# Hybrid decoder block on one core: four weight units instead of three during the first modulation, and the condition's row spread by TensorE

## The chip, the cores and the metric

The kernel runs on one core of a Trainium2 chip. The metric is device time in microseconds (us) of one execution, the median of several. Five engines run side by side, each through its own list of instructions in the order in which it was written: TensorE (PE, with its weight loads PEld), VectorE (DVE), ScalarE (ACT), GpSimd (POOL) and SyncE (SP), which here issues transfers. Each waits on semaphores for the others.

## The reference, cut to what matters

One layer with 512 tokens of width 1024. A conditioning vector `c` gives six vectors by one matrix product; the first two shift and scale the normed input of the token mixer.

```
mod = silu(c) @ ada_w + ada_b
shift1, scale1, gate1, shift2, scale2, gate2 = split(mod, 6)
h = rmsnorm(x, norm1_g) * (1 + scale1) + shift1
proj = h @ w_in + b_in                  # 512 + 2*512 + 2*1024 columns
  pool branch: trailing means of windows 2, 4, 8, 16, a map, a projection
  conv branch: a * sigmoid(a') -> causal depthwise conv, width 31 -> layer norm -> silu -> projection
x = x + gate1 * ((sigmoid(g1) * pool + sigmoid(g2) * conv) @ w_out)
h2 = rmsnorm(x, norm2_g) * (1 + scale2) + shift2
x = x + gate2 * peer(h2)                # 8 heads, top 16 of 128 x 128 product keys, 16384 experts
return rmsnorm(x, final_g)
```

## The kernel before, in words

Activations lie transposed: 8 chunks of 128 channels by 512 tokens. A weight unit is 128 output columns against all 1024 inputs, 128 x 1024 floats (512 KB). It is loaded by SP (`load_unit`, L112), cast to a 16-bit high part on ScalarE (`high`, L117) and to the 16-bit rest on VectorE (`low`, L123). The activation is split in the same way (`hhi`, `hlo`), and a product takes three matmuls (`mm3`, L170 to L172, or `unit`, L179): 24 of 512 columns for a unit. Loads, high and low parts have four buffers each, so the fifth high part needs the first one's buffer back from TensorE.

`w_in` has 28 units. The order of the list `order` begins 8, 4, 9, 5, 0: gate columns of the conv branch (sigmoid, L444), its values (`glu`, L448), and so on. `unit_out` treats a finished unit: it runs the sigmoid, the `glu` or the window sums, takes one step of the other four modulation vectors (`ada_step`: GpSimd multiplies a 512 KB block of `ada_t` with the row of silu(c), L371; ScalarE sums it, L372) and spends a budget of VectorE work from the list `fill`, which holds the depthwise conv, 31 instructions for each of four channel groups (L323, L327). All of it is written out in program order; no scheduler moves it.

The first units (`FU` = 3) are worked on while shift1 and scale1 arrive. For a quarter `q` of the channels, `start_rows(q)` multiplies silu(c), 32 columns wide (`cst`), with two blocks of 1 MB of `ada_n` (L284, `b` = 1 and then `b` = 0) and copies the sums out on ScalarE (L287). `start_turn(q)` turns that row into columns with four small matmuls (L294), and VectorE and ScalarE make `a1`, `shift1`, `hhi` and `hlo` for two chunks (L296 to L303). Then the three units use these two chunks, 6 matmuls each.

The row of silu(c) that GpSimd needs on all partitions, `crow`, is loaded as 128 copies of `c_row` (512 KB) and passed through Silu on ScalarE (L482) in the last quarter.

Of the kernel before, what the change touches and what calls it, by code (L numbers as in the profile page):

```python
# [7 lines left out]
F32 = mybir.dt.float32  # L8
# [3 lines left out]
AF = mybir.ActivationFunctionType  # L12
OP = mybir.AluOpType
# [3 lines left out]
P = 128  # L17
T = 512
D = 1024
NDC = D // P  # L20
# [20 lines left out]
SWE = 15  # L41
WSP = 0.25
ADAB = 3
FU = 3
BUD = 3.6
PL = ()
LNO = (1, 2, 3, 4, 5, 5, 6)
# [17 lines left out]
def body(tc, xt, cols, c_row, ada_n, ada_t, win, pool_w, pup, cvo, wout, wq, keys, ut, un, vn, fg, out, dbg=None):  # L65
    nc = tc.nc
    V, A, G, PE, SP = nc.vector, nc.scalar, nc.gpsimd, nc.tensor, nc.sync
# [11 lines left out]
    def bc_row(ap, n):  # L79
        return bass.AP(tensor=ap.tensor, offset=ap.offset, ap=[[0, P], [1, n]])  # L80
# [5 lines left out]
    def col(name):  # L86
        o, w = COLS[name]
        return colt[:, o:o + w]

    ident = const.tile([P, P], F32, name="ident")  # L90
# [10 lines left out]
    keyt = const.tile([P, 2, P], F32, name="keyt")  # L101
# [8 lines left out]
    def load_unit(src, bufs=4, pool=None):  # L110
        f = (pool or stream).tile([P, 1024], F32, name="unit_f", tag="f32", bufs=bufs)
        SP.dma_start(f, src)  # L112
        return f

    def high(f, scale, bufs=4, pool=None):
        hi = (pool or stream).tile([P, 1024], F16, name="unit_hi", tag="hi", bufs=bufs)
        A.activation(hi, f, AF.Copy, scale=scale)  # L117
        return hi

    def low(f, hi, scale, bufs=4, pool=None, eng=None):  # L120
        lo = (pool or stream).tile([P, 1024], F16, name="unit_lo", tag="lo", bufs=bufs)
        if eng is None:
            V.scalar_tensor_tensor(lo, f, scale, hi, op0=OP.mult, op1=OP.subtract)  # L123
        else:
            A.activation(f, f, AF.Copy, scale=scale)
            eng.tensor_tensor(lo, f, hi, op=OP.subtract)
        return hi, lo
# [7 lines left out]
    def run_ahead(n, nl=4, nh=3, ns=2):  # L135
        for j in range(n, min(n + nl, len(units))):
            if j not in loaded:
                loaded[j] = load_unit(units[j])
        for j in range(n, min(n + nh, len(units))):
            if j not in highs:  # L140
                highs[j] = high(loaded[j], WS)
        for j in range(n, min(n + ns, len(units))):
            if j not in halves:
                halves[j] = low(loaded[j], highs[j], WS, eng=G if j in PL else None)
# [7 lines left out]
    def lows_ahead():  # L152
        run_ahead(used[0], nl=0, nh=0, ns=2)
# [15 lines left out]
    def mm3(o, a, b, start, stop):  # L169
        PE.matmul(o, a[0], b[0], start=start, stop=False)  # L170
        PE.matmul(o, a[0], b[1], start=False, stop=False)  # L171
        PE.matmul(o, a[1], b[0], start=False, stop=stop)  # L172
# [13 lines left out]
    front = fs.enter_context(tc.tile_pool(name="front", bufs=1))  # L186
# [3 lines left out]
    def ps():  # L190
        return psf.tile([P, 512], F32, name="mm", tag="mm", bufs=4)

    def dense(rhs, p=None):
        hi, lo = next_unit()
        p = ps()
        unit(p, hi, lo, [slice(k * P, (k + 1) * P) for k in range(NDC)], rhs)
        return p

    crow = front.tile([P, D], F32, name="crow")

    cst = front.tile([P, NDC, 32], F32, name="cst")
    V.memset(cst, 0.0)
    A.activation(cst[:, :, 0], col("c"), AF.Silu)
    one = front.tile([P, 1], F32, name="one")
    V.memset(one, 1.0)
    mods = [const.tile([P, NDC], F32, name=f"mod{b}") for b in range(6)]
# [2 lines left out]
    def load_ada(u):  # L209
        f = front.tile([P, D], F32, name="ada_f", tag="ada_f", bufs=ADAB)  # L210
        SP.dma_start(f, ada_t[u - 2 * NDC])
        return f
# [35 lines left out]
    def start_load(u):  # L248
        SP.dma_start(spare[u % 5], ada_n[u].rearrange("p (k n) -> p k n", k=NDC))

    pn1 = psf.tile([P, 512], F32, name="ssq", tag="st", bufs=2)
    for k in range(0, NDC, 2):
        SP.dma_start(x_t[:, k:k + 2], xt[:, k:k + 2])
    run_ahead(0, nl=FU, nh=0, ns=0)
    for u in range(5):
        start_load(u)
    for k in range(NDC):
        sq = front.tile([P, 512], F32, name="sq", tag="rstd" if k == 0 else "sql", bufs=1 if k == 0 else 4)
# [4 lines left out]
            V.tensor_tensor(sq0, sq0, sq, op=OP.add)  # L263
    PE.matmul(pn1, ones_d, sq0, start=True, stop=False)
    PE.matmul(pn1, ones_d, sq, start=False, stop=True)
    run_ahead(0, nl=0, nh=FU, ns=FU)
    rstd = front.tile([P, 512], F32, name="rstd")
    A.activation(rstd, pn1, AF.Sqrt, bias=eps)
    b1 = front.tile([P, NDC], F32, name="b1")
# [3 lines left out]

    rows1 = {}

    def start_rows(q):

        p = ps_s.tile([P, 512], F32, name="s_ps", tag="s_ps", bufs=2)
        rows1[q] = front.tile([P, 512], F32, name="row", tag="df", bufs=2)
        for b in (1, 0):  # L280
            u = 2 * q + 1 - b
            for k in range(NDC):
                r = slice(32 * (k % 4), 32 * (k % 4) + 32)
                PE.matmul(p[r, b * 256:(b + 1) * 256], cst[:, k], spare[u % 5][:, k], start=(k < 4), stop=(k >= 4))  # L284
            if u + 5 < NDC:
                start_load(u + 5)
        A.activation(rows1[q], p, AF.Copy)  # L287

    def start_turn(q):

        row = rows1.pop(q)
        for c in range(4):
            b, k = c // 2, 2 * q + c % 2
            PE.matmul(pmod[:, b * NDC + k:b * NDC + k + 1], row[:, c * P:(c + 1) * P], one, start=True, stop=True)  # L294
        s = slice(2 * q, 2 * q + 2)
        V.tensor_tensor(shift1[:, s], pmod[:, s], col("ada_b")[:, s], op=OP.add)  # L296
        V.tensor_tensor(a1[:, s], pmod[:, NDC + 2 * q:NDC + 2 * q + 2], col("norm1_g")[:, s], op=OP.mult)
        V.tensor_tensor(a1[:, s], a1[:, s], b1[:, s], op=OP.add)
        for c in (2 * q, 2 * q + 1):
            V.scalar_tensor_tensor(sig[:, c], x_t[:, c], a1[:, c:c + 1], rstd, op0=OP.mult, op1=OP.mult)  # L300
            A.activation(hhi[:, c], sig[:, c], AF.Identity, bias=shift1[:, c:c + 1])
        for c in (2 * q, 2 * q + 1):
            V.scalar_tensor_tensor(hlo[:, c], sig[:, c], shift1[:, c:c + 1], hhi[:, c], op0=OP.add, op1=OP.subtract)  # L303
# [7 lines left out]
    pw = front.tile([P, 4, P], F32, name="pw")  # L311
# [50 lines left out]
    def ada_load():  # L362
        if nada[0] < 6 * NDC:
            adaf.append((nada[0], load_ada(nada[0])))
            nada[0] += 1
# [73 lines left out]
    def unit_out(n, p):  # L439
        j = order[n]  # L440
        budget = BUD
        if 8 <= j < 12:
            sg = gated[j - 8] = front.tile([P, T], F32, name="sg", bufs=2)
            A.activation(sg, p, AF.Sigmoid, scale=IWS, bias=bin_[:, j:j + 1])  # L444
        elif 4 <= j < 8:
            g = front.tile([P, PADC + T], F32, name="glu", bufs=4)
            G.memset(g[:, :PADC], 0.0)
            V.scalar_tensor_tensor(g[:, PADC:], p, bws[:, j - 4:j - 3], gated[j - 4], op0=OP.add, op1=OP.mult)  # L448
            fill.append(conv(j - 4, g))
            budget -= 0.7  # L450
        elif j < 4:
            wins[j] = windows(j, p)
            after(n + 2, do_df, j)
            after(n + 4, do_map, j)
        else:
            A.activation(sig[:, j - 12], p, AF.Sigmoid, scale=IWS, bias=bin_[:, j:j + 1])
        if n >= FU:
            lows_ahead()
        for f, a in at.get(n, []):
            f(*a)  # L460
            budget -= 0.8
        ada_step()
        ada_load()
        spend(budget, 2)
        if not fill and n > 12 and "c" not in lnorm:
            lnorm["c"] = n
            for k, f in zip(LNO, LN):
                after(n + k, f)
    V.reciprocal(rstd, rstd)
    used[0] = FU  # L470
    outs = [ps() for _ in range(FU)]
    start_rows(0)
    start_turn(0)
    start_rows(1)
    run_ahead(FU, nl=2, nh=0, ns=0)
    SP.dma_start(crow, bc_row(c_row, D))
    SP.dma_start(pw, pool_w)
    SP.dma_start(keyt, keys)
    ada_load()
    for q in range(4):  # L480
        if q == 3:
            A.activation(crow, crow, AF.Silu)  # L482
            run_ahead(FU, nl=2, nh=1, ns=1)
        for j in range(FU):
            hi, lo = halves[j]
            for k in (2 * q, 2 * q + 1):
                s = slice(k * P, (k + 1) * P)
                mm3(outs[j], (hi[:, s], lo[:, s]), (hhi[:, k], hlo[:, k]), k == 0, k == NDC - 1)
            if j == 0 and q < 3:
                start_turn(q + 1)  # L490
            if j == FU - 1 and q < 2:
                start_rows(q + 2)
            if q == 3:
                del halves[j]
                unit_out(j, outs[j])
    dump("hhi", hhi)
# [19 lines left out]
    for u in range(4):  # L516
        for jj, p in enumerate(half((mxhi, mxlo))):
            j = 2 * u + jj
# [16 lines left out]
    for u in range(4):  # L535
        for jj, p in enumerate(half((ychi, yclo))):
            j = 2 * u + jj
# [22 lines left out]
    for j in range(NDC):  # L560
        p = dense((mghi, mglo))
# [164 lines left out]
    for ch in range(17):  # L726
        if ch < 16:
            if ch < 2:
                p = firsts[ch]
            else:  # L730
                hi, lo = next_unit()
                p = q_tile()
# [226 lines left out]
    for g in range(NG):  # L959
        nxt = one_hots(g + 1) if g + 1 < NG else None  # L960
        n = left[0] // (NG - g)
# [253 lines left out]
```

## Time and profile before

| | us |
|---|---|
| median of 3 runs | 1474.02 (1470.59 to 1475.10) |
| profiled execution, its own time | 1472.85 |
| its span in the trace | 1471.1 |
| TensorE busy in it | 1412.7 (96%) |
| VectorE busy | 1270.3 (86%) |
| ScalarE busy | 669.9 (46%) |
| GpSimd busy | 458.3 (31%) |

The shares are means over stages. The change touches the first 60 us; the stage after it, up to about 184 us, is the projection `w_in` with the conv. In it the idle times of VectorE and of TensorE tell more than the shares over the span do. A row's number in brackets is the time that the engine stood idle before it, with what ended that.

### The profile page before, as it was taken

To read this page: it belongs to the slowest core of one execution; us is meant where nothing else is said; L and a number is where in the kernel's file an instruction comes from. 1 tells how busy PE (TensorE), PEld (TensorE's weight loads), DVE (VectorE), ACT (ScalarE), POOL (GpSimd) and SP (SyncE) were. 2 spreads that over 40 slices of the span, in tenths; PEclk is the share of its full clock that TensorE was granted. 3 is DMA by queue.
4 is the path that set the end of the run, shared out by engine and by line. 5 is a ranking of instruction groups with operands and counts; after the bars stand their busy time and mean duration, and the time that the engine had idled before them with its cause. 6 is when DMAs were issued, how large, how long until landed. Compare 5 with 4: busy or idle time off the path is not lost.

```text
span 1471.1 us, 21798 instructions
## 1 busy us (share of the span) xinstructions
PE 1412.7 (96%) x7969; PEld 743.1 (51%) x7969; DVE 1270.3 (86%) x2433; ACT 669.9 (46%) x931; POOL 458.3 (31%) x427
## 2 busy tenths in 40 slices
PE   6998999999989999999999999999999999999997
PEld 2443444445545666665555555555555555444443
DVE  6899966479999999958888988888888898899877
ACT  4554374343433788854333333333333333344334
POOL 0576443200000000000454544445445445422212
PEclk9999999999999999999999999999999999999998
DMA  9554533232233477794899999999999999999953
GB/s 386 192 194 172 185 123 137 79 136 87 72 113 129 150 268 269 249 297 174 295 381 364 371 365 361 375 362 358 366 343 377 364 363 342 357 359 337 326 206 134
DMA packets 145278, 386.79 MB, mean 263 GB/s; under 512 B 10897, under 2 KB 60305, under 8 KB 141073
## 3 DMA queue, kind: packets, MB, share of 16 engines
q1 hardware_dynamic: 108304, 251.15, 48.7%
q0 software_dynamic: 36864, 134.23, 24.8%
q8 instruction: 62, 1.02, 0.3%
q14 instruction: 48, 0.39, 0.1%
HBM read 355.98 MB, written 29.36 MB: 262 GB/s over the span
## 4 chain that ended last, share of the span: by engine, by line
PE 52%; DVE 28%; DMA 7%; issue 6%; POOL 4%; ACT 4%; SPq 0%; POOLq 0%; DVEq 0%; ACTq 0%
PE acc L1093 9%; PE acc L1095 9%; PE acc L1092 9%; DVE unit_lo L123 7%; PE s_ps L172 5%; PE s_ps L170 5%; PE s_ps L171 5%; PE mm L179 4%; DMA gat<-vn,eidx 4%; DVE s_ps L327 3%; POOL gat L987 2%; DVE oh L909 2%; DVE o L907 2%; DVE ol L910 2%; DMA unit_f<-ut 1%
## 5 line engine op out<-in xcount | busy, mean ns | idle before, releaser
L123 DVE SCALAR_TENSOR_TENSOR unit_lo<-unit_f,unit_hi 128x1024 f16<-128x1024 f32 x316 | 397.0, 1266 | 83.9 <-ACT unit_hi L117 80.9
L117 ACT ACTIVATE unit_hi<-unit_f 128x1024 f16<-128x1024 f32 x316 | 330.0, 1046 | 52.9 <-DMA unit_f<-ut 40.4
L987 POOL DMA_INDIRECT gat<-un,eidx x128 | 162.5, 1270 | 586.7 <-DVE bgate L826 421.8
L172 PE MATMUL s_ps<-h2hi,unit_lo 128*128 128x384 f16 x1024 | 334.5, 327 | 7.0 <-DVE unit_lo L123 7.0
L170 PE MATMUL s_ps<-h2hi,unit_hi 128*128 128x384 f16 x1024 | 334.6, 327 | 0.0
L171 PE MATMUL s_ps<-h2lo,unit_hi 128*128 128x384 f16 x1024 | 334.5, 327 | 0.0
L1092 PE MATMUL acc<-unit_hi,ghi 128*128 128x512 f16 x768 | 291.1, 379 | 0.6 <-ACT ghi L1042 0.6
L1093 PE MATMUL acc<-unit_lo,ghi 128*128 128x512 f16 x768 | 291.1, 379 | 0.4 <-DVE unit_lo L123 0.4
L1095 PE MATMUL acc<-unit_hi,glo 128*128 128x512 f16 x768 | 229.9, 379 | 0.1
L987 POOL DMA_INDIRECT gat<-vn,eidx x128 | 158.3, 1236 | 212.0 <-DVE bacc L1011 182.0
L1042 ACT ACTIVATE ghi<-g 128x384 f16<-128x384 f32 x128 | 67.0, 523 | 293.0 <-DVE g L1038 226.8
L1011 DVE SCALAR_TENSOR_TENSOR bacc<-gat,bw,bacc 128x1024 f32<-128x1024 f32 x127 | 162.6, 1280 | 14.9 <-DMA gat<-vn,eidx 14.0
L1003 DVE SCALAR_TENSOR_TENSOR gat<-gat,h2b 128x1024 f32<-128x1024 f32 x128 | 154.4, 1221 | 21.2 <-DMA gat<-un,eidx 20.7
L650 ACT ACTIVATE s_sb<-s_ps 128x384 f32<-128x384 f32 x128 | 63.0, 492 | 222.0 <-PE s_ps L172 211.3
L172 PEld LDWEIGHTS <-unit_lo 128*128 128x128 f16 x1176 | 115.5, 98 | 95.5 <-DVE unit_lo L123 9.2
L171 PEld LDWEIGHTS <-unit_hi 128*128 128x128 f16 x1176 | 115.4, 98 | 85.8 <-issue 3.7
L170 PEld LDWEIGHTS <-unit_hi 128*128 128x128 f16 x1176 | 115.7, 98 | 84.6 <-issue 3.2
L1095 PEld LDWEIGHTS <-glo 128*128 128x128 f16 x768 | 75.0, 98 | 91.6 <-DVE glo L1045 1.5
L1092 PEld LDWEIGHTS <-ghi 128*128 128x128 f16 x768 | 75.1, 98 | 88.4 <-ACT ghi L1042 1.6
L1093 PEld LDWEIGHTS <-ghi 128*128 128x128 f16 x768 | 75.1, 98 | 86.2
L179 PEld LDWEIGHTS <-unit_hi 128*128 128x128 f16 x656 | 64.2, 99 | 91.3 <-ACT unit_hi L117 9.1
L371 POOL TENSOR_TENSOR ada_f<-ada_f,crow 128x1024 f32<-128x1024 f32 x32 | 86.0, 2705 | 69.3 <-ACT crow L482 42.9
(229 smaller groups left out, 1689.4 us busy)
## 6 DMA issues: line engine op xcount, KB each, us to landing
unit_f<-ut SPq DMA_DIRECT2D x128, 512.0 KB
unit_f<-vn SPq DMA_DIRECT2D x128, 512.0 KB
wd<-wst SPq DMA_DIRECT2D x24, 1024.0 KB
wr<-wd SPq DMA_DIRECT2D x16, 1536.0 KB
ada_f<-ada_t SPq DMA_DIRECT2D x32, 512.0 KB
unit_f<-win SPq DMA_DIRECT2D x28, 512.0 KB
unit_f<-wq SPq DMA_DIRECT2D x16, 512.0 KB
sig<-ada_n SPq DMA_DIRECT2D x4, 1024.0 KB
```

Of the source, the lines that this page charges most:

```text
L117: A.activation(hi, f, AF.Copy, scale=scale)
L123: V.scalar_tensor_tensor(lo, f, scale, hi, op0=OP.mult, op1=OP.subtract)
L170: PE.matmul(o, a[0], b[0], start=start, stop=False)
L171: PE.matmul(o, a[0], b[1], start=False, stop=False)
L172: PE.matmul(o, a[1], b[0], start=False, stop=stop)
L179: PE.matmul(p, w[:, s], r[:, k], start=(i == 0 and k == 0), stop=(i == 2 and k == n - 1))
L987: G.indirect_dma_start(out=t, out_offset=None, in_=un if n < HK else vn, in_offset=bass.IndirectOffsetOnAxis(ap=bs["eidx"][:, k:k + 1], ax ...
L1003: V.scalar_tensor_tensor(t, t, 1.0, h2b, op0=OP.mult, op1=OP.mult, accum_out=bs["pre"][:, n:n + 1])
L1011: V.scalar_tensor_tensor(bacc, t, bw[:, k:k + 1], bacc, op0=OP.mult, op1=OP.add)
L1092: PE.matmul(acc[t][h], ghi[:, ts_], vhi[:, h * 512:(h + 1) * 512], start=st, stop=False)
L1093: PE.matmul(acc[t][h], ghi[:, ts_], vlo[:, h * 512:(h + 1) * 512], start=False, stop=False)
L1095: PE.matmul(acc[t][h], glo[:, ts_], vhi[:, h * 512:(h + 1) * 512], start=False, stop=sp)
```

## The change: what it does

`FU` becomes 4, so four units share the quarters. Two units are loaded ahead of the first two `ada_n` blocks, two behind them; the high and low parts of the third and fourth are made after the first quarter's modulation instead of before it. Four more units are queued behind the last `ada_n` block, ahead of `pw`, `keyt` and the `ada_t` blocks. `crow` is no longer loaded: VectorE writes diag(silu(c)) into it, and TensorE multiplies it with a tile of ones (`spread`, eight matmuls of 128 columns in two halves); ScalarE copies the result back. The first half stands between the two halves of `start_rows(0)`, the second behind the small matmuls of `start_turn(0)`. `start_rows(q + 1)` now stands behind the first unit of quarter `q`, `start_turn(q + 1)` behind the second. In the last quarter the parts of units 4 and 5 are written behind the matmuls of units 0 and 1.

```diff
-FU = 3
+FU = 4
     A.activation(cst[:, :, 0], col("c"), AF.Silu)
+    V.tensor_tensor(crow.rearrange("p (k n) -> p k n", k=NDC), cst[:, :, 0:1].to_broadcast([P, NDC, P]),
+                    ident[:, None, :].to_broadcast([P, NDC, P]), op=OP.mult)
...
+    run_ahead(0, nl=2, nh=0, ns=0)
+    start_load(0)
+    start_load(1)
     run_ahead(0, nl=FU, nh=0, ns=0)
-    for u in range(5):
+    for u in range(2, 5):
         start_load(u)
...
-    run_ahead(0, nl=0, nh=FU, ns=FU)
+    run_ahead(0, nl=0, nh=2, ns=2)
...
     V.reciprocal(rstd, rstd)
     used[0] = FU
     outs = [ps() for _ in range(FU)]
-    start_rows(0)
-    start_turn(0)
-    start_rows(1)
-    run_ahead(FU, nl=2, nh=0, ns=0)
-    SP.dma_start(crow, bc_row(c_row, D))
-    SP.dma_start(pw, pool_w)
-    SP.dma_start(keyt, keys)
-    ada_load()
+    ones = front.tile([P, P], F32, name="ones", tag="pt", bufs=2)
+    V.memset(ones, 1.0)
+    def spread(h):
+        for k in range(4 * h, 4 * h + 4):
+            PE.matmul(outs[2 + h][:, k % 4 * P:(k % 4 + 1) * P], ones, crow[:, k * P:(k + 1) * P], start=True, stop=True)
+    start_rows(0, spread)
+    start_turn(0, spread)
+    for h in range(2):
+        A.activation(crow[:, h * 512:(h + 1) * 512], outs[2 + h], AF.Copy)
+    run_ahead(0, nl=0, nh=FU, ns=FU)
     for q in range(4):
-        if q == 3:
-            A.activation(crow, crow, AF.Silu)
-            run_ahead(FU, nl=2, nh=1, ns=1)
         for j in range(FU):
             hi, lo = halves[j]
...
-            if j == 0 and q < 3:
+            if q < 3 and j == 0:
+                start_rows(q + 1)
+                if q == 0:
+                    run_ahead(FU, nl=4, nh=0, ns=0)
+                if q == 1:
+                    SP.dma_start(pw, pool_w)
+                    SP.dma_start(keyt, keys)
+                    ada_load()
+            if q < 3 and j == 1:
                 start_turn(q + 1)
-            if j == FU - 1 and q < 2:
-                start_rows(q + 2)
             if q == 3:
+                if j < 2:
+                    run_ahead(FU, nl=2, nh=j + 1, ns=j + 1)
```

How TensorE's list begins, before (-) and now (+): `s_ps` is the sum of `start_rows`, `pmod` the small matmuls, `mm<-crow,ones` the spread.

```order
-L284 MATMUL s_ps<-sig,cst 32x256 x16
-L294 MATMUL pmod<-one,row 128x1 x4
-L284 MATMUL s_ps<-yc,cst 32x256 x8
-L284 MATMUL s_ps<-h2hi,cst 32x256 x8
+L290 MATMUL s_ps<-sig,cst 32x256 x8
+L489 MATMUL mm<-crow,ones 128x128 x4
+L290 MATMUL s_ps<-sig,cst 32x256 x8
+L302 MATMUL pmod<-one,row 128x1 x4
+L489 MATMUL mm<-crow,ones 128x128 x4
 L170 LDWEIGHTS unit_hi
 L170 MATMUL mm<-hhi,unit_hi 128x512
```

The sums of the second quarter (`yc`, `h2hi`) have moved behind the first unit's matmuls, and the spread stands among those of the first quarter.

VectorE's list at the same place, with what each instruction waits for. Now:

```order
L276 SCALAR_TENSOR_TENSOR b_170<-colt 128x8 [waits DMAHW0_49]
L317 TENSOR_SCALAR dwk<-colt 128x124
L319 TENSOR_SCALAR bws<-colt 128x4
L479 RECIPROCAL rstd<-rstd 128x512 [waits Activation_49]
L484 MEMSET ones 128x128
L306 TENSOR_TENSOR mod_108<-pmod,colt 128x2 [waits PE_49]
```

Before, L296 (now L306) followed the reciprocal directly; the tile of ones is new, and it is written behind the reciprocal.

The end of the last quarter on ScalarE: `sg` is the first unit's sigmoid, `ada_f` a summing step. Before:

```order
L482 ACT_TABLE_LOAD
L482 ACTIVATE crow<-crow 128x1024 [waits DMAHW2_49]
L117 ACTIVATE unit_hi<-unit_f 128x1024 [waits DMAHW0_49]
L444 ACT_TABLE_LOAD
L444 ACTIVATE sg<-mm,colt 128x512 [waits PE_49]
```

Now:

```order
L117 ACTIVATE unit_hi<-unit_f 128x1024 [waits DMAHW1_49,PE_49]
L454 ACT_TABLE_LOAD
L454 ACTIVATE sg<-mm,colt 128x512 [waits PE_49]
L382 ACTIVATE ada_f,mod_110<-ada_f 128x1024 [waits Pool_49]
L117 ACTIVATE unit_hi<-unit_f 128x1024 [waits DMAHW2_49,PE_49]
L382 ACTIVATE ada_f,mod_110<-ada_f 128x1024 [waits Pool_49]
```

The Silu is gone, and both high parts, those of units 4 and 5, now wait for TensorE (for the buffers of units 0 and 1); before, the one high part there waited for its transfer alone. On VectorE the two low parts stand ahead of the first `glu` (L458); before, one did (`L123`, then L448).

## Rows read from the trace of the kernel before

**Rows 1.** The page's first line: span and instructions.
```profile
span 1471.1 us, 21798 instructions
```

**Rows 2.** Stages: start to end, length, busy us of each engine, clock, DMA share, GB/s.
```profile
40.00:50.00 10.00, 9.99 (x51) 5.00 (x50) 6.03 (x9) 7.49 (x9) 3.71 (x3) 1.00 0.07 26
100.00:180.00 80.00, 74.73 (x337) 32.94 (x335) 79.31 (x97) 39.04 (x60) 47.23 (x27) 1.00 0.52 177
180.00:190.00 10.00, 7.82 (x31) 3.26 (x32) 6.60 (x7) 5.71 (x10) 3.42 (x2) 1.00 0.32 92
```

**Rows 3.** Timeline of VectorE: start, us, line, operation; in brackets idle before.
```profile
16.07 3.35 DVE L469 RECIPROCAL rstd<-rstd 128x512 f32<-128x512 f32 x1 [0.48 <-ACT rstd L268]
...
29.89 1.42 DVE L303 SCALAR_TENSOR_TENSOR hlo<-sig,mod,hhi 128x512 f16<-128x512 f32 x2
...
47.18 2.54 DVE L123 SCALAR_TENSOR_TENSOR unit_lo<-unit_f,unit_hi 128x1024 f16<-128x1024 f32 x1 [2.56 <-ACT unit_hi L117]
49.64 0.74 DVE L448 SCALAR_TENSOR_TENSOR glu<-mm,bws,sg 128x512 f32<-128x512 f32 x1
...
59.13 1.22 DVE L123 SCALAR_TENSOR_TENSOR unit_lo<-unit_f,unit_hi 128x1024 f16<-128x1024 f32 x1
...
60.92 1.22 DVE L123 SCALAR_TENSOR_TENSOR unit_lo<-unit_f,unit_hi 128x1024 f16<-128x1024 f32 x1
...
71.00 1.24 DVE L123 SCALAR_TENSOR_TENSOR unit_lo<-unit_f,unit_hi 128x1024 f16<-128x1024 f32 x1 [0.41 <-ACT unit_hi L117]
...
87.49 2.70 DVE L123 SCALAR_TENSOR_TENSOR unit_lo<-unit_f,unit_hi 128x1024 f16<-128x1024 f32 x1 [0.41 <-ACT unit_hi L117]
```

**Rows 4.** Timeline of TensorE, the first 60 us.
```profile
13.09 1.91 PE L265 MATMUL ssq<-sq,ones_d 128*128 128x512 f32 x2
...
17.97 1.07 PE L284 MATMUL s_ps<-sig,cst 128*32 128x256 f32 x16 [0.97 <-DMA sig<-ada_n]
19.75 1.05 PE L294 MATMUL pmod<-one,row 128*128 128x1 f32 x8 [0.72 <-ACT row L287]
...
22.95 1.70 PE L284 MATMUL s_ps<-h2hi,cst 128*32 128x256 f32 x16 [1.14 <-DMA h2hi<-ada_n]
24.57 0.61 PE L170 MATMUL mm<-hhi,unit_hi 128*128 128x512 f16 x1
...
26.90 0.95 PE L294 MATMUL pmod<-one,row 128*128 128x1 f32 x8
27.71 0.38 PE L170 MATMUL mm<-hhi,unit_hi 128*128 128x512 f16 x1
...
30.39 1.07 PE L284 MATMUL s_ps<-h2lo,cst 128*32 128x256 f32 x16
...
47.69 1.89 PE L179 MATMUL mm<-hhi,unit_hi 128*128 128x512 f16 x8
...
51.14 1.89 PE L179 MATMUL mm<-hhi,unit_lo 128*128 128x512 f16 x8
56.43 2.69 PE L179 MATMUL mm<-hhi,unit_hi 128*128 128x512 f16 x8 [3.40 <-ACT unit_hi L117]
```

**Rows 5.** Timeline of ScalarE, the first 60 us.
```profile
14.05 1.28 ACT L268 ACT_TABLE_LOAD   x1
15.35 0.69 ACT L268 ACTIVATE rstd<-ssq,eps 128x512 f32<-128x512 f32 x1
...
22.09 1.38 ACT L301 ACTIVATE hhi<-sig,mod 128x512 f16<-128x512 f32 x2 [2.39 <-DVE sig L300]
...
48.46 0.69 ACT L444 ACTIVATE sg<-mm,colt 128x512 f32<-128x512 f32 x1
49.05 1.05 ACT L372 ACTIVATE ada_f<-ada_f 128x1024 f32<-128x1024 f32 x1
```

**Rows 6.** Chain of waits at 291 us: start, length, what.
```profile
291.30 2.60 PE nat L586 x20
```

**Rows 7.** Timeline of GpSimd, from 40 us.
```profile
46.28 2.35 POOL L371 TENSOR_TENSOR ada_f<-ada_f,crow 128x1024 f32<-128x1024 f32 x1 [42.85 <-ACT crow L482]
```

More of the change, by code (lines that the diff above doesn't have):

```diff
@@ L274, in body, with start_rows @@
     rows1 = {}
-    def start_rows(q):
+    def start_rows(q, wait=None):
         p = ps_s.tile([P, 512], F32, name="s_ps", tag="s_ps", bufs=2)
@@ L284, in start_rows @@
                 PE.matmul(p[r, b * 256:(b + 1) * 256], cst[:, k], spare[u % 5][:, k], start=(k < 4), stop=(k >= 4))
+            if wait and b:
+                wait(0)
             if u + 5 < NDC:
@@ L287, in start_rows, with start_turn @@
         A.activation(rows1[q], p, AF.Copy)
-    def start_turn(q):
+    def start_turn(q, wait=None):
         row = rows1.pop(q)
@@ L294, in start_turn @@
             PE.matmul(pmod[:, b * NDC + k:b * NDC + k + 1], row[:, c * P:(c + 1) * P], one, start=True, stop=True)
+        if wait:
+            wait(1)
         s = slice(2 * q, 2 * q + 2)
```

## The prediction

> **What bounds the kernel now.** I read the stages first, then the timelines of the engines over the first 60 us. From 100 to 180 us VectorE is busy 79.31 of 80 us, TensorE 74.73, ScalarE 39.04 [rows 2]: the projection stage is VectorE's, and this holds until its busy share falls, in 180 to 190 us (6.60 of 10). The reader is to see that this begins much earlier. The first `glu` on VectorE starts at 49.64 us with no idle before it, and after it the timeline shows two waits of 0.41 us, at 71.00 and 87.49 [rows 3]. So from 49.64 us on VectorE works through the conv and the low parts almost without a pause, and the end of the stage lies as late as that start plus the work behind it. TensorE's visible loss, 3.40 us of idle at 56.43 and then matmuls that ran slower (8 in 2.69 us against 1.89) [rows 4], lies beside this run of VectorE. Whoever removes it gains only if VectorE also begins earlier or has less to do. What the change is worth is therefore the start of the first `glu`, less the VectorE work taken out from behind it.
>
> **The start, step by step.** The order shows that the first half of the spread stands on TensorE between the two halves of the first sums, and that it needs the tile of ones, which VectorE writes behind the reciprocal. Both lists run in order, so nothing passes it.
>
> The last matmul of the norm runs from 13.09 for 1.91 us, to 15.0 [rows 4]. The square root started at 15.35, behind a table load from 14.05 to 15.33 [rows 5]; with one high part less ahead of it (1.05 us, the size of the row at 49.05 [rows 5]) the table is loaded by 14.3, and the root can start at 15.05. Its 0.69 us [rows 5], the reciprocal's 3.35 [rows 3] and some 0.2 for the fill give ones at 19.3 us. TensorE waits there. The four products are eight passes; the nearest row with 128 x 128 floats has 20 passes in 2.60 us, 0.13 each [rows 6], so 1.05 us, to 20.4. Then the second half of the sums, 1.07 us, which before started at 17.97 when its transfer landed [rows 4]: it ends at 21.5 instead of 19.04. One unit less is loaded ahead of these blocks; two blocks of 1 MB landed between 17.97 and 22.95 [rows 4], so 512 KB are 1.25 us. That is thus worth nothing: the second block is there at 16.7 and waits for the spread. The second half of the spread (1.05 us) costs nothing; it lies in the 3.05 us between the sums' end (19.04) and the first `hhi` (22.09 [rows 5]), of which the small matmuls take 1.05.
>
> Before, the second quarter's sums came next and ended at 24.57, where the first unit began [rows 4]. Now the first unit goes ahead of them. From the sums' end to the start of the small matmuls are 0.71 us (19.04 to 19.75 [rows 4]); from that start to the end of the two `hlo` 4.4 us (26.90 on TensorE, 29.89 + 1.42 on VectorE [rows 3, 4]). So `hlo` is whole at 26.6, the first unit's six matmuls end at 27.0, the second quarter's sums (two times 1.07 [rows 4]) at 29.1, the second unit's six at 30.4; a matmul costs 0.216 us, from 16 between 47.69 and 51.14 [rows 4]. ScalarE in the meantime copies `crow` back (twice the 0.69 us of 512 columns) and makes two high parts (twice 1.05), all behind `hhi`, which ends at 25.95: it is free at 29.4 and copies the second row by 30.1, just in time. VectorE's two low parts lie in its wait, too.
>
> **The quarters.** A quarter now takes 24 matmuls (5.18 us), its sums (2.1), the gap that the small matmuls make (26.90 to 27.71, 0.81 [rows 4]): 8.1 us. The way round from the small matmuls to the end of `hlo` is 4.4 us against 3.4 of matmuls and gap before the next quarter begins and 4.26 before it needs the last `hlo`; I add 0.05. The small matmuls of quarters 1 and 3 start at 30.4 and 46.7, and the first unit ends 4.4 + 0.4 us later, at 51.5.
>
> One more thing lies in this stretch. `crow` is ready at 27, so GpSimd no longer waits until 46.28 for it [rows 7]; it multiplies as soon as the first `ada_t` block lands. The bytes up to there are those that before had landed by about 40.7 (the transfers fill 0.07 of 40 to 50 us [rows 2]; one 512 KB broadcast is gone, one unit more is loaded ahead, and two more stand before the first of these blocks). The multiplies of 2.35 us thus run from 40.7 to about 48, and VectorE makes `sig` and `hlo` of the third quarter from 40 to 43. The low part at 47.18, begun 0.9 us into such a multiply, took 2.54 us instead of 1.22 [rows 3, 7], 1.3 more. From below the collision costs 0, from above the rest of one multiply, 2.35; I take 1.5, nearest to the row, and the first unit ends at 53.0.
>
> The Trainium skill ("SBUF — State Buffer", section "Who interferes with whom") says that a VectorE instruction with two SBUF inputs contends with a GpSimd instruction that reads SBUF, and that the loser blocks for the whole of the other. By it a collision costs up to the full 2.35 us, and the sum would be 0.85 higher; the low part at 47.18, which ends 1.1 us after the multiply, agrees [rows 3, 7]. By the same section the conv's instructions, whose running sum is in PSUM, lose nothing to GpSimd, so that starting the multiplies early gives nothing back there.
>
> **The end of the quarters.** Before, the Silu with its two table loads delayed the first sigmoid to 48.46. That goes, but the four buffers are now all in work: high(4) waits for the first unit's end, and VectorE's order puts low(4) and low(5) ahead of the first `glu`. From 53.0 on ScalarE: high(4) 1.05, a table load 1.28, the sigmoid 0.59 (48.46 to 49.05), the summing step 1.1, high(5) 1.05 [rows 5]; then low(5), 1.22 [rows 3]: 6.3 us, so the first `glu` starts at 59.3 instead of 49.64, 9.7 later. Less two low parts that before stood behind it (59.13 and 60.92, 1.15 from start to next start, 2.3 [rows 3]), less the two waits of 0.41, since ScalarE then has a lead over VectorE: 9.7 - 2.3 - 0.8 = 6.6 us later at the end of the stage. TensorE's removed idle time should come back as a wait for low parts. Behind the stage nothing is taken out, and what follows waits for the conv; I give back nothing. `crow`'s diag on VectorE lies in its wait for the squares, the four queued loads in transfers that would come anyway.
>
> **The sum.** The profiled execution took 1472.85 us, its span 1471.1 [rows 1], 1.75 around it, which stays; with 6.6 it is 1479.5. The median of the runs is 1.2 above the profiled one; on it the sum is 1480.6. I predict 1480.0.
>
> **Rivals.** First, TensorE sets the end. For it speaks its 74.73 of 80 us [rows 2] and that the 3.40 us and the slow matmuls are real. Then what counts is when the fifth unit ends: before at 63.3 (56.43, 24 matmuls, and 1.7 for the slow clock, worked out in the third rival); now four units end at 53.0 + 3.9 and the fifth, without a wait, at 62.1: 1.2 less, 1471.7 to 1472.8. Had the spread not held the start back (5.2 us, the second rival), 1467. Against it: VectorE's 79.31 of 80 us. It decides where the low parts are ready before TensorE asks for them.
>
> Second, the spread holds nothing up (ones or root come earlier than I reckon). Sums end at 17.8, the first unit at 47.8 with no collision, the first `glu` at 54.1: 4.5 - 3.1 = +1.4, 1475.4. Against it: the order. For it: nothing but that ends of matmuls are modelled.
>
> Third, worse: the clock falls inside the quarters. After 1.14 us of idle the sums at 22.95 took 1.70 us instead of 1.07, and the six matmuls from 24.57 to 26.90 2.33 instead of 1.29, in all 1.7 us; after 3.40 us of idle, eight took 2.69 instead of 1.89 [rows 4]. TensorE now stands idle for over 2 us before 19.3, and again before its first matmul. If the slow stretch falls where TensorE is the limit, 1.7 us come on top, and a second blocked multiply 2.35: 1484.
>
> **Chances.** The forecast 0.55, and its own range, from no collision to a full one and with 1.5 for errors in the chain, 1477 to 1483; TensorE sets the end 0.17; the spread free 0.13; worse 0.15. The range that should hold 8 in 10 reaches down into the first rival and takes in the third: 1472.5 to 1485.5. A measurement of this kernel tells about 0.3% from no change, 4.4 us: slower is above 1478.4. Of the forecast 0.43 lies above that and 0.12 below; of the worst case 0.13 above, 0.02 below; the free spread is no change, at 0.13; TensorE's case is no change with the start held back (0.09) and faster without (0.08). That makes faster 0.08, same 0.36, slower 0.56.
>
> **What would show it.** TensorE idle before the spread until about 19.3; the sums' second half at about 20.4; the first unit's matmuls from about 25; the first `glu` at 58 to 60.5; VectorE full from there to about 190, where now it is 184; TensorE waiting for low parts at unit 6. A first `glu` before 56, or a VectorE with pauses of more than 3 us behind it, would make the prediction wrong.

## The result, and the profile after

The changed kernel takes 1485.11 us (median of 4 runs, 1483.72 to 1487.49) against 1474.56 (4 runs, 1470.59 to 1475.34) for the kernel before: a ratio of 1.0075, 95% interval 1.0057 to 1.0094. It is slower by 10.5 us. Forecast were 1480.0 us and a range of 1472.5 to 1485.5. The direction held, and so did the engine that sets the end; two prices on the way to it did not, and the loss is nearly twice the forecast.

The span, and two stages of it (start to end, length, busy us of TensorE, its weight loads, VectorE, ScalarE, GpSimd, then granted clock, DMA share, GB/s):

```profile
span 1483.0 us, 21832 instructions
```

```profile
100.00:180.00 80.00, 76.39 (x337) 33.19 (x336) 79.57 (x101) 40.24 (x61) 49.91 (x33) 0.98 0.53 183
180.00:190.00 10.00, 10.00 (x48) 4.42 (x46) 9.79 (x14) 5.71 (x9) 1.83 (x3) 1.00 0.53 178
```

VectorE still fills the projection stage (79.57 of 80 us), and where it was falling off, at 180 to 190, it now works 9.79 of 10 us [rows 2]. The stage only lies later. Its timeline shows from where:

```profile
16.03 3.35 DVE L479 RECIPROCAL rstd<-rstd 128x512 f32<-128x512 f32 x1 [1.11 <-ACT rstd L274]
19.36 0.17 DVE L484 MEMSET ones<- 128x128 f32 x1
...
44.39 5.38 DVE L313 SCALAR_TENSOR_TENSOR hlo<-sig,mod,hhi 128x512 f16<-128x512 f32 x2
...
58.14 1.41 DVE L313 SCALAR_TENSOR_TENSOR hlo<-sig,mod,hhi 128x512 f16<-128x512 f32 x2
61.11 1.23 DVE L123 SCALAR_TENSOR_TENSOR unit_lo<-unit_f,unit_hi 128x1024 f16<-128x1024 f32 x1 [1.56 <-ACT unit_hi L117]
65.09 1.23 DVE L123 SCALAR_TENSOR_TENSOR unit_lo<-unit_f,unit_hi 128x1024 f16<-128x1024 f32 x1 [2.75 <-ACT unit_hi L117]
66.23 0.75 DVE L458 SCALAR_TENSOR_TENSOR glu<-mm,bws,sg 128x512 f32<-128x512 f32 x1
```

The first `glu` starts at 66.23 instead of 49.64 [rows 3], 16.6 us later, and behind it VectorE stands idle no more than 0.16 us at a time up to the conv's end. In the third quarter two `hlo` that usually take 1.41 took 5.38. GpSimd's timeline at that moment:

```profile
43.73 2.75 POOL L381 TENSOR_TENSOR ada_f<-ada_f,crow 128x1024 f32<-128x1024 f32 x1 [40.29 <-DVE sig L310]
46.42 0.12 POOL L457 MEMSET glu<- 128x30 f32 x1
46.49 5.49 POOL L381 TENSOR_TENSOR ada_f<-ada_f,crow 128x1024 f32<-128x1024 f32 x2
```

The three multiplies, which began at 46.28 before [rows 7], now begin at 43.73 and cover the two `hlo` from 44.39 on. TensorE's timeline:

```profile
15.20 1.67 PE L290 MATMUL s_ps<-sig,cst 128*32 128x256 f32 x16
19.57 1.82 PE L489 MATMUL mm<-crow,ones 128*128 128x128 f32 x8 [2.70 <-DVE ones L484]
21.33 1.94 PE L290 MATMUL s_ps<-sig,cst 128*32 128x256 f32 x16
...
29.53 0.63 PE L172 MATMUL mm<-hhi,unit_lo 128*128 128x512 f16 x1
...
33.27 0.95 PE L302 MATMUL pmod<-one,row 128*128 128x1 f32 x8
...
41.41 0.95 PE L302 MATMUL pmod<-one,row 128*128 128x1 f32 x8
...
47.07 0.38 PE L171 MATMUL mm<-hlo,unit_hi 128*128 128x512 f16 x1 [1.89 <-DVE hlo L313]
...
49.83 0.38 PE L171 MATMUL mm<-hlo,unit_hi 128*128 128x512 f16 x1 [1.94 <-DVE hlo L313]
50.35 1.74 PE L290 MATMUL s_ps<-sig,cst 128*32 128x256 f32 x16
51.84 1.95 PE L290 MATMUL s_ps<-yc,cst 128*32 128x256 f32 x16
...
55.16 0.95 PE L302 MATMUL pmod<-one,row 128*128 128x1 f32 x8
```

Three things are to be seen. TensorE waits 2.70 us for the ones, as forecast. What follows the wait is slow: the sums at 21.33 take 1.94, against 1.07 at full clock [rows 4]. And the period of the quarters, 8.14 us from 33.27 to 41.41, becomes 13.75 from there to 55.16.

### The profile page after: what moved, and what is told of

It reads as the page before. It is cut to its first block, busy times and chain, and to the rows that moved or that the text cites. A ratio compares the mean times of both kernels' runs of the same rounds, so it can differ in the third digit from the quotient of the medians.

```text
span 1483.0 us, 21832 instructions
## 1 busy us (share of the span) xinstructions
PE 1421.3 (96%) x7985; PEld 746.1 (50%) x7985; DVE 1274.1 (86%) x2435; ACT 668.9 (45%) x931; POOL 455.4 (31%) x427
## 4 chain that ended last, share of the span: by engine, by line
PE 57%; DVE 29%; DMA 5%; issue 4%; ACT 3%; POOL 2%; SPq 0%; DVEq 0%; ACTq 0%; POOLq 0%
PE acc L1116 9%; PE acc L1114 9%; PE acc L1113 9%; DVE unit_lo L123 7%; PE s_ps L172 6%; PE s_ps L170 6%; PE s_ps L171 6%; DVE s_ps L337 5%; PE mm L179 3%; DMA gat<-vn,eidx 2%; DVE oh L930 2%; DVE ol L931 2%; DVE o L928 2%; ACT unit_hi L117 1%; PE q_ps L171 1%
## 5 line engine op out<-in xcount | busy, mean ns | idle before, releaser
L123 DVE SCALAR_TENSOR_TENSOR unit_lo<-unit_f,unit_hi 128x1024 f16<-128x1024 f32 x316 | 396.6, 1265 | 85.6 <-ACT unit_hi L117 84.9
L381 POOL TENSOR_TENSOR ada_f<-ada_f,crow 128x1024 f32<-128x1024 f32 x32 | 82.5, 2595 | 83.4 <-DMA ada_f<-ada_t 43.1
```

## Experiments

All in the table but the changed kernel were timed in five rounds beside the kernel before. "Conv end" is the start of ScalarE's copy of the last conv sum. The row for the changed kernel is that of the first section.

| kernel | first `glu` at | conv end | median us (runs) | ratio to before, 95% |
|---|---|---|---|---|
| before | 49.64 | 184.29 | 1474.25 (23); 1473.67 (23); 1473.38 (15) | |
| changed | 66.23 | 198.35 | 1485.11 (4) | 1.0075 (1.0057 to 1.0094) |
| ones early | 59.06 | 190.95 | 1478.03 (12) | 1.0024 (1.0014 to 1.0033) |
| GpSimd held | 60.97 | 193.59 | 1481.46 (6) | 1.0041 (1.0026 to 1.0057) |
| before, VectorE late | 64.45 | 200.78 | 1490.52 (5) | 1.0107 (1.009 to 1.0123) |
| before, TensorE late | 49.78 | 188.28 | 1475.72 (12) | 1.0011 (1.0001 to 1.0021) |
| early, parts behind | 54.44 | 189.99 | 1477.05 (9) | 1.0031 (1.002 to 1.0043) |
| held, clock kept | 57.79 | 190.88 | 1479.49 (6) | 1.0046 (1.0031 to 1.0061) |
| three units | 47.15 | 182.10 | 1468.32 (9) | 0.9969 (0.9957 to 0.9982) |
| two units | 45.60 | 181.86 | 1469.06 (12) | 0.9967 (0.9956 to 0.9977) |
| four units, all remedies | 51.73 | 187.34 | 1474.03 (11) | 1.0005 (0.9996 to 1.0014) |

**Which engine sets the end: VectorE late, TensorE late.** Both start from the kernel before. One puts 12 instructions on VectorE ahead of the first `glu`, the other the matmuls of one more unit on TensorE. The added work changes no value that the kernel uses.

```diff
+            if n == 1:
+                for _ in range(12):
+                    V.tensor_tensor(rstd, rstd, rstd, op=OP.max)
             V.scalar_tensor_tensor(g[:, PADC:], p, bws[:, j - 4:j - 3], gated[j - 4], op0=OP.add, op1=OP.mult)
```

```diff
     for n in range(FU, len(order)):
+        if n == 5:
+            x = psf.tile([P, 512], F32, name="extra", tag="st", bufs=2)
+            for i in range(24):
+                PE.matmul(x, hhi[:, i % NDC, :P], hhi[:, i % NDC], start=(i == 0), stop=(i == 23))
         unit_out(n, dense((hhi, hlo)))
```

> The kernel before the change with one edit: twelve extra instructions of VectorE (128 x 512, about 0.65 us each, 8 us in all, more where GpSimd blocks them) ahead of the first glu; nothing else is touched. Theory (VectorE sets the end of the projection stage): the first glu starts 8 us or more later than 49.6 and the time grows by the same amount, to about 1482.5. Rival (TensorE sets the end, VectorE has room): the time grows by less than 3 us.

> The kernel before the change with one edit: 24 extra matmuls of 512 columns (5.2 us) on TensorE ahead of the sixth unit. Theory (TensorE has room in the projection stage): the time stays within 1.5 us of the kernel before. Rival (TensorE sets the end, as the removal of its 3.4 us of idle time would need): the time grows by about 5 us, to 1479.7.

VectorE's 12 instructions, then TensorE's 24 matmuls, and VectorE's two longest waits in the run with these:

```profile
49.65 14.88 DVE L450 TENSOR_TENSOR rstd<-rstd 128x512 f32<-128x512 f32 x12
```

```profile
63.27 5.34 PE L501 MATMUL extra<-hhi 128*128 128x512 f16 x24
```

```profile
79.08 0.75 DVE L448 SCALAR_TENSOR_TENSOR glu<-mm,bws,sg 128x512 f32<-128x512 f32 x1 [0.73 <-PE mm L179]
...
92.23 2.69 DVE L123 SCALAR_TENSOR_TENSOR unit_lo<-unit_f,unit_hi 128x1024 f16<-128x1024 f32 x1 [2.52 <-ACT unit_hi L117]
```

14.88 us on VectorE moved the first `glu` by 14.8, the conv's end by 16.5 and the time by 16.3. The 12 took longer than was reckoned for them: the first three, beside GpSimd's multiplies, 2.72 to 2.83 us each, the others, behind these, 0.69; the shift is read from what they took. 5.34 us on TensorE moved the median by 1.5 (0.15 to 3.1). The traced execution, at 1479.65 the longest of the 12, shows more: there the conv's end lies 4.0 later, and VectorE waits 0.73 us for a `glu`'s matmuls and 2.52 for a high part. So VectorE sets the end, and TensorE has room for part of the 5.34 us: by the median for most of it, by this trace for far less. The rival in which TensorE sets the end, so that all of the 5.34 us comes out in the time, falls; how soon still more work on TensorE would make it the bound stays open.

**The wait for the ones.** The changed kernel, with the tile of ones filled at the start, in a buffer of its own, instead of behind the reciprocal:

```diff
+    ones = front.tile([P, P], F32, name="ones")
+    V.memset(ones, 1.0)
     one = front.tile([P, 1], F32, name="one")
...
-    ones = front.tile([P, P], F32, name="ones", tag="pt", bufs=2)
-    V.memset(ones, 1.0)
```

> The changed kernel with one edit: the tile of ones is filled at the start, ahead of the squares, instead of behind the reciprocal. Theory (the first glu on VectorE sets the end of the projection stage, one for one): TensorE no longer stands at 16.9 to 19.6 us, the first quarter's sums end about 3.2 us earlier, at 20 instead of 23.3, and if the two blocked hlo of the third quarter cost the same 4 us as now, the first glu starts at 63 instead of 66.2 and the time falls by about 3.2 us, to 1482. Rival (the start's wait is given back at the third quarter, where the multiplies of GpSimd run at a fixed time set by the transfers): the glu stays within 1 us of 66 and so does the time. Second rival (TensorE sets the end): the glu moves and the time does not.

The time fell by 7.1 us and the first `glu` came 7.2 earlier, twice what was expected. TensorE no longer waits for the ones, and the spread and the sums run at full speed; then, below, the third quarter's `hlo` on VectorE and GpSimd's first multiply:

```profile
16.17 1.16 PE L489 MATMUL mm<-crow,ones 128*128 128x128 f32 x8
17.26 1.07 PE L292 MATMUL s_ps<-sig,cst 128*32 128x256 f32 x16
```

```profile
39.82 1.42 DVE L315 SCALAR_TENSOR_TENSOR hlo<-sig,mod,hhi 128x512 f16<-128x512 f32 x2
```

```profile
42.61 2.36 POOL L383 TENSOR_TENSOR ada_f<-ada_f,crow 128x1024 f32<-128x1024 f32 x1 [39.17 <-DMA ada_f<-ada_t]
```

The `hlo` are over at 41.24 and the multiply begins at 42.61, when its transfer lands: this collision is gone too. The early ones removed two terms at once, since the `hlo` came 4.6 us earlier (44.39 to 39.82) and GpSimd's first multiply, which waits for a transfer, only 1.1 (43.73 to 42.61). But the multiplies now meet the fourth quarter's two `sig`:

```profile
47.38 3.46 DVE L312 SCALAR_TENSOR_TENSOR sig<-x_t,mod,rstd 128x512 f32<-128x512 f32 x2
```

The next two runs take the collision and the clock one after the other.

**The collision alone.** The changed kernel, with one copy on GpSimd that reads the last `hlo` and so holds its multiplies until then:

```diff
     for q in range(4):
+        if q == 3:
+            held = front.tile([P, 1], F32, name="held")
+            G.tensor_copy(held, hlo[:, NDC - 1, 0:1])
         for j in range(FU):
```

> The changed kernel with one edit: GpSimd first copies one column of the last hlo of the fourth quarter, so that its multiplies of ada_t blocks begin only when VectorE has made all hlo. Theory: the two hlo of the third quarter take 1.4 us again instead of 5.4, TensorE does not stand there and its slow sums behind it (1.5 us) go as well; the first glu starts 4 to 5.5 us earlier, at 61 to 62, and the time falls by as much, to 1480 to 1481. Rival (the multiplies are late now and hold up ScalarE's summing steps and high parts behind them): the glu moves little, or VectorE waits later for high parts, and the time falls by less than 2 us.

```profile
44.52 1.41 DVE L313 SCALAR_TENSOR_TENSOR hlo<-sig,mod,hhi 128x512 f16<-128x512 f32 x2
```

The `hlo` of the third quarter take 1.41 again and the first `glu` comes 5.26 earlier, as expected; the time falls by 3.65, a little less than the 4 to 5.5 expected.

**The clock alone.** The kernel just told of, with ten matmuls, whose result is overwritten, in TensorE's wait for the ones:

```diff
+        if h == 0:
+            for i in range(10):
+                PE.matmul(outs[0], halves[0][0][:, :P], halves[0][0][:, :512], start=True, stop=True)
         for k in range(4 * h, 4 * h + 4):
```

> The version with GpSimd held, and ten matmuls of 512 columns, whose results nobody reads, between the first half of the sums and the spread, while TensorE would wait for the ones. Theory (the low granted clock behind that wait lengthens the spread, the second half of the sums and the first unit): the eight spreads take about 1.05 us and the second half of the sums 1.07 (1.8 and 1.94 with GpSimd held alone), the first glu starts 1.5 to 2 us before 60.97, and the time is about 1479.5 to 1480 (1481.46). Rival (the low clock there is hidden by other engines): first glu and time as with GpSimd held alone.

The spread and the sums behind it, with GpSimd held alone and then in this run:

```profile
19.28 1.22 PE L489 MATMUL mm<-crow,ones 128*128 128x128 f32 x8 [2.44 <-DVE ones L484]
20.43 1.94 PE L290 MATMUL s_ps<-sig,cst 128*32 128x256 f32 x16
```

```profile
19.09 1.16 PE L492 MATMUL mm<-crow,ones 128*128 128x128 f32 x8 [0.31 <-DVE ones L484]
20.18 1.07 PE L290 MATMUL s_ps<-sig,cst 128*32 128x256 f32 x16
```

Stages of 4 us with the granted clock as the third number from the end, of the changed kernel, then with GpSimd held alone, then of this run:

```profile
18.00:22.00 4.00, 2.42 (x16) 1.93 (x20) 1.52 (x2) 0.00 (x0) 0.00 (x0) 0.74 1.03 426
...
26.00:30.00 4.00, 2.74 (x7) 0.65 (x5) 2.71 (x5) 3.69 (x6) 0.00 (x0) 0.59 1.01 422
...
52.00:56.00 4.00, 4.00 (x35) 2.04 (x28) 0.00 (x0) 0.60 (x1) 0.05 (x1) 0.75 0.00 0
```

```profile
22.00:26.00 4.00, 3.28 (x17) 2.92 (x14) 0.95 (x4) 0.60 (x1) 0.00 (x0) 0.50 1.02 424
26.00:30.00 4.00, 3.66 (x11) 1.25 (x9) 2.71 (x5) 3.77 (x6) 0.00 (x0) 0.50 1.01 420
```

```profile
18.00:22.00 4.00, 2.97 (x29) 1.58 (x27) 1.04 (x2) 0.60 (x1) 0.00 (x0) 1.00 1.03 427
22.00:26.00 4.00, 2.54 (x18) 2.04 (x19) 2.75 (x7) 1.70 (x3) 0.00 (x0) 1.00 1.01 422
26.00:30.00 4.00, 4.00 (x42) 1.73 (x41) 2.83 (x3) 3.14 (x5) 0.00 (x0) 1.00 1.01 422
```

In the changed kernel TensorE spent part of each of these stretches at the lower of its two levels, 1.2 instead of 2.4 GHz, after it had waited, and with GpSimd held alone all of 22 to 30 us; with the wait filled it stays at full clock. In this pair of traces the spread itself hardly changes (1.22 us and 1.16; the 1.8 of the expectation is the changed kernel's); what gains are the sums (1.94 to 1.07) and what follows them. The first `glu` comes 3.18 us earlier than with GpSimd held alone, and the time falls by 1.97 (1481.46 to 1479.49). The ones come no earlier here, so this is the price of the clock behind the wait; what the wait costs by its own length no run shows alone. With early ones the small matmuls of quarter 1 start another 1.5 us earlier (28.69 against 30.22).

The length of a wait alone does not tell whether the clock falls. TensorE's waits for the first and the last quarter's `hhi` in the run with early ones, and the stretches around them:

```profile
22.15 0.38 PE L170 MATMUL mm<-hhi,unit_hi 128*128 128x512 f16 x1 [1.06 <-ACT hhi L313]
...
50.98 0.38 PE L170 MATMUL mm<-hhi,unit_hi 128*128 128x512 f16 x1 [2.44 <-ACT hhi L313]
```

```profile
22.00:26.00 4.00, 3.44 (x18) 1.06 (x21) 2.71 (x5) 3.62 (x6) 0.00 (x0) 0.57 1.01 422
...
50.00:54.00 4.00, 2.61 (x12) 1.12 (x12) 2.32 (x5) 2.52 (x4) 0.00 (x0) 1.00 0.00 0
```

Behind 1.06 us the granted clock was 0.57, behind 2.44 us it stayed at 1.00; and in the run with the clock kept the same wait for the first `hhi`, 1.05 us, was followed by 1.00.

**The parts of units 4 and 5.** Early ones, and the two high and low parts written behind the second unit's output:

```diff
             if q == 3:
-                if j < 2:
-                    run_ahead(FU, nl=2, nh=j + 1, ns=j + 1)
                 del halves[j]
                 unit_out(j, outs[j])
+                if j == 1:
+                    run_ahead(FU, nl=2, nh=2, ns=2)
```

> The early ones, and the high and low parts of units 4 and 5 written behind the second unit's output instead of ahead of the first. Theory (the start of the first glu moves the end one for one): on ScalarE and VectorE one high part, one wait for it and one low part go from ahead of the first glu, so that it starts at about 54.3 us where the early ones alone had 59.06; the two low parts that now stand behind it give 2.3 us of this back: time about 1475.5 to 1476, 2 to 2.5 us under the early ones alone (1478.03). Rival (TensorE then waits for the low part of unit 4, so that nothing is gained): the first glu starts earlier, but the time stays at 1478.

The first `glu` came 4.62 earlier, as expected, but the conv's end and the time only by 1.0. VectorE's timeline from the first `glu` on, and then a wait of TensorE:

```profile
54.44 0.75 DVE L460 SCALAR_TENSOR_TENSOR glu<-mm,bws,sg 128x512 f32<-128x512 f32 x1 [2.05 <-PE mm L172]
...
59.19 4.08 DVE L123 SCALAR_TENSOR_TENSOR unit_lo<-unit_f,unit_hi 128x1024 f16<-128x1024 f32 x2
```

```profile
62.19 1.90 PE L179 MATMUL mm<-hhi,unit_lo 128*128 128x512 f16 x8 [1.72 <-DVE unit_lo L123]
```

The two low parts are back behind it, and beside one of GpSimd's multiplies (58.70, 2.35 us) they take 4.08 us, not the 2.3 expected. TensorE waits 1.72 us for one of them, as the rival said, but VectorE waits no more than 0.2 us behind its first `glu`. A start of `glu` that only changes places with other VectorE work is no gain; the rule "one for one" holds for the same work behind it.

**Fewer units.** From the kernel before: three units as before, the spread with early ones instead of the loaded `crow`, the next parts and the sigmoid's table load in the third quarter, GpSimd held. The two-unit version differs in `FU` = 2, and in two further buffers for the spread. Of the edit, the part in the quarters (the spread is left out):

```diff
...
     for q in range(4):
+        if q == 2:
+            run_ahead(FU, nl=4 - FU, nh=4 - FU, ns=4 - FU)
+            A.activation(warm, eps, AF.Sigmoid)
         if q == 3:
-            A.activation(crow, crow, AF.Silu)
-            run_ahead(FU, nl=2, nh=1, ns=1)
+            held = front.tile([P, 1], F32, name="held")
+            G.tensor_copy(held, hlo[:, NDC - 1, 0:1])
```

> The kernel before with three units in work, as it had, condition's row spread by TensorE from early ones, the parts of the next unit written in the third quarter, the sigmoid table loaded there, and GpSimd's multiplies held until the last low half of the shifts. Theory (the start of the first glu moves the end one for one): the table load and one high and low part go from ahead of the first glu: it starts at about 46.5 us (before 49.64), and the time falls by about 3 to 1471. Rival (TensorE sets the end of the stage, or the moved parts delay the quarters by as much): 1474 or more.

> The same as the three-unit version, with two units in work while the first shift and scale arrive, and the parts of units 2 and 3 written in the third quarter. Theory: each quarter is shorter by one unit's six matmuls, and the first unit ends at about 42.3 us; the first glu starts at about 43.7 to 44 us, 5.5 us before that of the kernel before, and the time falls to about 1468.7. Rival (TensorE sets the end, and the work that it doesn't do in the quarters comes behind): 1474 or more.

Both beat the kernel before by 0.3% and do not differ from each other. With three units the first `glu` starts at 47.15, where the expectation said 46.5; the conv's end lies 2.2 earlier than before and the median 5.4 lower, so that the start of the `glu` does not explain the whole gain (some of it may lie in the stage told of under the rest of the span). With two units the `glu` starts at 45.60, later than the 43.7 to 44 expected, and the conv's end is only 0.24 earlier than with three. The stretch from 48 to 72 us, three units and then two, and a wait of VectorE in the latter:

```profile
48.00:72.00 24.00, 22.58 (x106) 10.07 (x105) 23.64 (x29) 15.05 (x23) 15.91 (x11) 1.00 0.79 285
```

```profile
48.00:72.00 24.00, 24.00 (x113) 10.89 (x112) 22.10 (x31) 12.56 (x19) 15.70 (x11) 1.00 0.63 227
```

```profile
68.15 1.25 DVE L123 SCALAR_TENSOR_TENSOR unit_lo<-unit_f,unit_hi 128x1024 f16<-128x1024 f32 x1 [1.41 <-ACT unit_hi L117]
```

With three units VectorE is full there (23.64 of 24 us), with two TensorE is (24.00), and VectorE waits. Here the rival seems to set in: two units put so little of TensorE's work in front that it becomes the bound for a while. That is read from these rows; no run tests it.

**Four units with all remedies.** Early ones and parts behind, as above, and in addition the table load in the third quarter and GpSimd held:

```diff
     for q in range(4):
+        if q == 2:
+            A.activation(warm, eps, AF.Sigmoid)
+        if q == 3:
+            held = front.tile([P, 1], F32, name="held")
+            G.tensor_copy(held, hlo[:, NDC - 1, 0:1])
         for j in range(FU):
```

> Four units in work with every remedy found so far: early ones, the parts of units 4 and 5 behind the first glu, the sigmoid table loaded in the third quarter, GpSimd's multiplies held until the last low half of the shifts. Theory (the start of the first glu moves the end one for one, and a fourth unit in the quarters costs what its own matmuls take): the fourth quarter's low halves follow the third's by the undisturbed period, 8.15 us, instead of 10.26, so that the first glu starts at about 52.3 us (54.44 without the last two remedies) and the time is about 1475, some 6 us over the three-unit version (glu at 47.15, 1468.3). Rival (the faults of the change lay in its waits alone, and four units are as good as three): 1470 or less.

The first `glu` at 51.73 and 1474.03 us, no different from the kernel before (1.0005). Against the three-unit version it is 4.6 us later at the `glu` and 5.2 at the conv's end. With the faulty waits in the quarters gone, most of that is what the fourth unit costs: from the third quarter's `hlo` to the fourth's it is 8.15 us here (40.12 to 48.27) and 6.66 in the kernel before (36.54 to 43.20), where three units share a quarter. Four times the difference of 1.49 is 6.0. It is not the fourth unit alone: the two versions also differ in where the spread and the next parts are written, and the four-unit trace has a wait of TensorE of 2.58 us for a high part, at 56.79.

**The rest of the span.** From the conv's end to the end of the span are 1286.8 us before and 1284.7 in the changed kernel, so 2.1 of the 14.1 were given back. ScalarE's copies in the stage that builds the rows' weights, in the profiles of before, of before once more, and of the changed kernel (count, shortest, median, longest in ns, first and last start in us):

```profile
L927 ACT ACTIVATE wst<-w_ps x96: 1027/1073/1129, 493.1 to 638.4; 128x512 f32<-128x512 f32 x96
```

```profile
L927 ACT ACTIVATE wst<-w_ps x96: 1030/1081/1130, 493.2 to 637.0; 128x512 f32<-128x512 f32 x96
```

```profile
L948 ACT ACTIVATE wst<-w_ps x96: 1027/1077/1124, 506.9 to 650.5; 128x512 f32<-128x512 f32 x96
```

> The kernel before, unchanged, for a second profile. The stage that builds the weights of the gathered rows took 145.3 us in its first profile (493.1 to 638.4), and 143.5 to 143.6 in the profiles of the changed kernel and of the three-unit version. If that difference of 1.8 us belongs to the order of the work before it, it stands at 145.3 again; if it differs from one execution to the next, it can come out at 143.5.

The second profile of the unchanged kernel (1472.02 us) has 143.8 us there, the first 145.3, the changed kernel 143.6. So for one and the same kernel it differs from one execution to the next. In the profiles of the eight kernels with the spread it was 143.5 or 143.6 each time, and with the two that keep the old start 145.6 and 143.6; whether the old order makes the longer case likelier stays open. The medians give back more (14.1 at the conv's end, 10.5 in the time), and why is open too.

## Why the prediction was right in kind and wrong in size

- **VectorE sets the end:** right. 14.88 us on it cost 16.3, 5.34 us on TensorE cost 1.5 in the median, 4.0 at the conv's end of its trace.
- **Ones at 19.3, TensorE waits:** right; the spread starts at 19.57, after 2.70 us.
- **Spread 1.05, sums 1.07, first unit's matmuls 0.216 each:** this step failed, and made 2.9 us. The prices were those of a TensorE at full clock, put behind a wait that the same paragraph foretold. Measured were 1.76 from the spread's start to that of the sums, then 1.94, and 0.43 from matmul to matmul (28.68 to 29.11). The small matmuls of quarter 1 started at 33.27, not 30.4. The rows of before already had the price (sums of 1.70 after 1.14 us idle), and it stood in the third rival, where it was given 0.15. The run with the clock kept gained 3.2 us at the first `glu`.
- **Quarter period 8.15:** right, 8.14.
- **Collision +1.5, from above 2.35:** the other failed step, and made 4.1 us. It was priced as one blocked instruction. Two `hlo` were blocked, 3.97 us over their 1.41, by multiplies that followed each other almost without a gap (they were forecast from 40.7 and ran from 43.73), and TensorE's two waits of 1.9 us then slowed the sums of the next quarter (1.95 at 51.84). In all the third quarter grew by 5.6; holding GpSimd gained 5.26. The Trainium skill ("SBUF — State Buffer", section "Who interferes with whom") says that of VectorE and GpSimd the one that issues first has their shared port pair for the whole instruction and that the other blocks. For two instructions that bounds the loss by two multiplies, an estimate of 4.7 us, and the 3.97 agree. That one instruction loses at most one multiply was right; the count was not. The three added instructions beside the multiplies in the run with VectorE late show the same price, about 2.0 us each (2.72 against 0.69). GpSimd lost as well: 8.24 us for three multiplies that take 7.00 with early ones (2.36 and 4.64), where the last two meet the `sig` and lose nothing.
- **6.3 us from the first unit's end to the `glu`:** right, 6.2 (60.02, where ScalarE begins the high part, to 66.23). Moving the parts of units 4 and 5 behind it, in the pair of runs with early ones, took 4.6 off.
- **-3.1 behind the `glu`:** 132.1 us from `glu` to conv end instead of 134.65, so -2.5. Nearly right.
- **Nothing given back behind the stage:** 2.1 us were in the profiled executions, 3.5 in the medians. Without that the miss would have been larger: the forecast had 6.6 at the conv's end, and it was 14.1.

The two failed steps make up the miss at the first `glu`: 2.9 and 5.6 - 1.5 = 4.1 are 7.0, and it came at 66.23 instead of 59.3, 6.9 later.

The worse case of the prediction, slow clock and a second blocked multiply at 1484 us, is what happened. It was treated as two mishaps, when both seem to follow from the wait that the forecast itself held for certain: the wait lowers the clock, the low clock delays the quarters by 2.9 us, and that delay brings the third quarter's `hlo` wholly under GpSimd's multiplies. The first two links are shown by the run with the clock kept. The last is read from two runs and not shown by one of its own: with the clock kept (and GpSimd held) these `hlo` run from 41.35 to 42.77, and with early ones the first multiply begins at 42.61. The second rival, the spread free, came out at 1478.0 when it was built, not the 1475.4 given for it, and its first `glu` at 59.06 instead of 54.1. Two us of that were there at the small matmuls of quarter 1 (28.69, where that rival's chain gives 26.7), mostly since the first unit again ran at 0.43 us per matmul; three came in the fourth quarter, where the two `sig` meet the multiplies (3.46 us instead of 1.42) and TensorE waits 2.44 us behind them.

## What to carry to other kernels

A wait on TensorE can cost more than its length, because what runs behind it may run at half clock (0.50 here); if you forecast the wait, work out the next rows at the slow price too, and give it more than a small chance. When a step shifts one of two engines that block each other, as VectorE and GpSimd do here, lay the two timelines over each other again, and count every instruction that falls under the other's run. More work in flight ahead of the first result is a loss once the engine that sets the end waits for that result: here the best version with four units was slower than the one with three (1474.03 and 1468.32), and with two the bound seems to pass to TensorE for a while.

## What was not expected of the hardware

Two `hlo` beside GpSimd's back-to-back multiplies took 5.38 us instead of 1.41, and both sides lost (GpSimd 8.24 instead of 7.00); two `sig` beside the same multiplies took 3.46 instead of 1.42, and there GpSimd lost nothing. Ten matmuls in a wait for the ones (2.70 us in the changed kernel) were worth 3.18 us at the first `glu` and 1.97 in the time, though nobody reads what they compute. A wait of 2.44 us left the clock at 1.00 in one place, and one of 1.06 us was followed by 0.57 in another.
